# Transposing attention probabilities in fewer, larger groups

## The chip, the cores and the metric

The kernel runs on one core of one Trainium2 chip. The metric is the device time of one execution in microseconds (us). A core has five engines with a queue each: PE (TensorE, matmul and the loading of its weights, which the profile lists apart as PEld), ACT (ScalarE), DVE (VectorE), POOL (GpSimd) and SP (SyncE, which issues most of the DMA). The profile of one execution gives, for each instruction, its start, its duration and what it waited for.

## The reference

Two transformer blocks over 512 tokens and 1024 features, in float32. In order: a gated feed-forward layer; a mixer with two attentions side by side (a "forgetting" causal attention with 8 heads, and a "native sparse" one with 8 heads that adds a compressed, a selected and a windowed branch; at 512 tokens the selected and the windowed branch both come out as full causal attention); attention to 256 memory tokens with 4 heads of 256; a second feed-forward layer; sliding-window attention with sinks (16 heads, window 128); a pooling layer. Cut to what matters here, each attention is

```python
sc = jnp.einsum('bhqd,bkhd->bhqk', qi, k) + bias          # scores
p = masked_softmax(sc, mask)                               # rows are queries
o = jnp.einsum('bhqk,bkhd->bqhd', p.astype(v.dtype), v)    # products with the values
```

with a triangular mask in the mixer, none for the memory tokens, and a band of 128 in the window layer.

## The kernel before, in words

Activations lie feature-major, `[128 features, 512 tokens]`. Each large matmul is done three times to keep float32 accuracy: a number is split into a high part (ACT rounds it, L78) and a low part (DVE subtracts, L81), and `three` (L117 to L119) adds high*high, high*low and low*high. Weights come by DMA as `wr`, and are split into `wh` and `wl`; `wr`, `wh` and `wl` have three buffers each.

PSUM, where PE writes, has eight banks of `[128, 512]` in four pairs: `mm` (the large matmuls), `sc` (scores), `tr` (transposes, and a second bank for some matmuls) and `pv` (products with the values). Each name has two buffers: a third tile of that name waits until one of the two has been read for the last time.

An attention head is a `Unit` with three lists of steps: *scores*, *turns* and *products*. The probabilities come out of the softmax with queries on the partitions; for the product with the values they must have keys there. A *turn* transposes 128x128 blocks on PE into a `tr` bank, and ACT and DVE split that bank into `ph` and `pl`. A *product* multiplies `ph` and `pl` with the values.

- A causal unit (`causal_unit`, 24 of them: 8 in the forgetting attention, "fox", 16 in the native sparse one, "nsa") has four score steps, one for each block of 128 queries. Its four turns are one for each block j of 128 keys; only the blocks i >= j exist, so turn j has 4, 3, 2 or 1 transposes (L430) and its `ph` is 512, 384, 256 or 128 wide. Its four products (L442, L443) have two matmuls each.
- A memory unit (`mem_unit`, 4 of them) has two score steps and two turns of four transposes (L1015); all its product matmuls stand in its second product.
- A window unit (`swa_unit`, 16 of them) has two score steps, two turns of four and three transposes (L1193), and two products of eight and eight matmuls (L1209).

`run` sets the order on PE, by slots. One slot is: some steps of other work ("backlog": the matmuls of projections and gates that come later), one score step, at most one turn that has come due, some more backlog, at most one product that has come due. A unit's turns come due `lag` (2) slots after its last score, minus one, plus the unit's own `later`; a product comes due `hold` slots after its turn (1 in fox and in the memory layer, 2 in nsa and in the window layer). The backlog that is left is spread evenly over the slots that are left; `tail` says how many slots are counted on after the last score (6 in fox and nsa). `run` ends when no turn and no product is left. Work that is in the backlog then stays there, and goes out in the next `run` that has the same backlog; fox and nsa share one (`log` in `mixer`).

PE executes in exactly the order that is written. The order on ACT, DVE and POOL is made by a scheduler from the dependencies.

Other turns of the same kind in nsa: a unit for the compressed branch (`nsa_units`: L851 transposes its scores into a `tr` bank, which DVE reads at L853).

## Time and profile before

| | |
|---|---|
| median of 3 runs | 1718.14 us (1717.2 to 1718.44) |
| the profiled execution | 1718.07 us |
| its span, first to last instruction | 1716.3 us |
| outside the span | 1.8 us |
| granted TensorE clock, mean | 0.998 |
| busy: PE, PEld, DVE, ACT, POOL | 98%, 81%, 57%, 44%, 14% |
| fox run / nsa run / window run | about 438 to 548 / 573 to 745 / 1405 to 1512 us |
| the end of the memory run | 932 us |

A matmul's duration in the profile is the time from its start to the (modelled) end of its last write; consecutive matmuls overlap. What a matmul costs is therefore the distance from its start to the start of the next one: 0.23 us for a 512-wide matmul in a steady stream that has a duration of 0.40. A figure in square brackets behind a row is the idle time of the engine just before that instruction, and the instruction that ended it.

### The profile page before, as it was taken

The numbers are of one execution on the slowest core, as the hardware profiler recorded it, in microseconds if no ns is written. First come the engines' busy times: TensorE is split into PE (matmuls) and PEld (weight loads), VectorE is DVE, ScalarE is ACT, GpSimd is POOL, SyncE is SP. The second block draws the span as 40 slices with busy tenths as digits, with TensorE's granted clock in tenths as the row PEclk, the third lists the DMA queues.
The fourth block names the chain that finished last, engine by engine and source line by source line (L and its number), as shares of the span: only waits on it lengthen the run. The fifth ranks groups of instructions, "written<-read, shape, count | busy, mean of one in ns | idle before, by whom it ended". The sixth has DMA issues, their size and how long they took to land.

```text
span 1716.3 us, 22080 instructions
## 1 busy us (share of the span) xinstructions
PE 1683.8 (98%) x8300; PEld 1390.8 (81%) x8300; DVE 976.4 (57%) x1726; ACT 753.8 (44%) x1352; POOL 246.2 (14%) x323
## 2 busy tenths in 40 slices
PE   8999999999999999999999999999999999999997
PEld 5888878888787888887988888888888888878887
DVE  6343433336786677776655443433333698876674
ACT  6222222225675566645534432222223477744342
POOL 2000000003322232203001200000011044420001
PEclk9999999999999999999999999999999999999999
DMA  5222244433343122135521522222344311143232
GB/s 196 96 89 98 91 139 121 128 115 96 109 138 113 56 74 80 32 123 198 189 93 61 183 87 99 88 97 97 91 128 126 126 62 62 62 142 120 92 117 77
DMA packets 66256, 184.19 MB, mean 107 GB/s; under 512 B 7980, under 2 KB 13884, under 8 KB 66149
## 3 DMA queue, kind: packets, MB, share of 16 engines
q1 hardware_dynamic: 59300, 171.25, 30.9%
q10 hardware_dynamic: 6848, 11.54, 1.8%
q8 instruction: 65, 1.06, 0.2%
q14 instruction: 43, 0.34, 0.1%
HBM read 170.14 MB, written 15.24 MB: 108 GB/s over the span
## 4 chain that ended last, share of the span: by engine, by line
PE 88%; DVE 6%; ACT 2%; POOL 1%; issue 1%; DMA 0%; SPq 0%; DVEq 0%; ACTq 0%; POOLq 0%
PE mm L117 20%; PE mm L118 20%; PE mm L119 20%; PE tr L119 6%; PE tr L118 6%; PE tr L117 6%; PE tr L430 1%; PE pv L321 1%; DVE wl L81 1%; PE pv L322 1%; PE pv L323 1%; PE pv L443 1%; PE sc L403 1%; DVE pl L81 1%; PE pv L442 1%
## 5 line engine op out<-in xcount | busy, mean ns | idle before, releaser
L78 ACT ACTIVATE wh<-wr 128x1024 fp32r<-128x1024 f32 (+2 forms) x292 | 294.5, 1009 | 665.7 <-PE mm L118 351.4
L81 DVE TENSOR_TENSOR wl<-wr,wh 128x1024 fp32r<-128x1024 f32 (+2 forms) x291 | 342.5, 1178 | 172.9 <-ACT wh L78 168.7
L117 PE MATMUL mm<-xh,wh 128*128 128x512 f32 x872 | 358.3, 411 | 6.9 <-ACT wh L78 6.0
L118 PE MATMUL mm<-xl,wh 128*128 128x512 f32 x872 | 347.4, 398 | 0.9 <-DVE xl L89 0.7
L119 PE MATMUL mm<-xh,wl 128*128 128x512 f32 x872 | 346.3, 397 | 0.0
L223 POOL TENSOR_TENSOR acc<-acc,t 128x512 f32<-128x512 f32 (+1 forms) x55 | 75.3, 1376 | 958.8 <-ACT t L222 958.6
L117 PEld LDWEIGHTS mm<-xh,wh 128*128 128x128 f32 x872 | 166.0, 190 | 39.1 <-ACT wh L78 6.5
L119 PEld LDWEIGHTS mm<-xh,wl 128*128 128x128 f32 x872 | 164.8, 189 | 39.3 <-DVE wl L81 0.2
L118 PEld LDWEIGHTS mm<-xl,wh 128*128 128x128 f32 x872 | 165.5, 190 | 33.8 <-DVE xl L89 3.5
L119 PE MATMUL tr<-xh,wl 128*128 128x512 f32 x424 | 168.3, 397 | 0.5 <-DVE wl L81 0.5
L117 PE MATMUL tr<-xh,wh 128*128 128x512 f32 x424 | 168.2, 397 | 0.0
L118 PE MATMUL tr<-xl,wh 128*128 128x512 f32 x424 | 168.2, 397 | 0.0
L117 PE MATMUL mm<-hh,wh 128*128 128x512 f32 x352 | 139.0, 395 | 0.0
L119 PE MATMUL mm<-hh,wl 128*128 128x512 f32 x352 | 139.0, 395 | 0.0
L118 PE MATMUL mm<-hl,wh 128*128 128x512 f32 x352 | 139.0, 395 | 0.0
L356 DVE TENSOR_TENSOR t<-t,tr 128x512 f32<-128x512 f32 x44 | 30.2, 687 | 143.9 <-PE tr L119 142.5
L119 PEld LDWEIGHTS tr<-xh,wl 128*128 128x128 f32 x424 | 79.9, 189 | 20.3 <-DVE wl L81 0.9
L118 PEld LDWEIGHTS tr<-xl,wh 128*128 128x128 f32 x424 | 79.9, 189 | 19.4
L117 PEld LDWEIGHTS tr<-xh,wh 128*128 128x128 f32 x424 | 79.9, 188 | 19.3
L353 DVE TENSOR_TENSOR t<-mm,rstd 128x512 f32<-128x512 f32 x44 | 30.4, 691 | 112.4 <-PE mm L119 112.4
L81 DVE TENSOR_TENSOR pl<-tr,ph 128x512 fp32r<-128x512 f32 (+3 forms) x136 | 72.1, 530 | 24.0 <-ACT ph L78 23.1
L78 ACT ACTIVATE ph<-tr 128x512 fp32r<-128x512 f32 (+3 forms) x136 | 63.0, 466 | 50.8 <-PE tr L430 44.1
(346 smaller groups left out, 3000.8 us busy)
## 6 DMA issues: line engine op xcount, KB each, us to landing
wr<-in_f2gu_dram SPq DMA_DIRECT2D x44, 512.0 KB, 3.2
wr<-in_f1gu_dram SPq DMA_DIRECT2D x42, 512.0 KB, 3.3
wr<-in_mfm_dram SPq DMA_DIRECT2D x32, 512.0 KB, 3.2
xd<-xs ACTq DMA_DIRECT2D x40, 256.0 KB, 2.0
wr<-in_ain_dram SPq DMA_DIRECT2D x18, 512.0 KB, 3.2
wr<-in_f1d_dram SPq DMA_DIRECT2D x16, 512.0 KB, 3.7
xs<-xd SPq DMA_DIRECT2D x32, 256.0 KB, 3.3
wr<-in_f2d_dram SPq DMA_DIRECT2D x16, 512.0 KB, 3.6
```

Of the source, the lines that this page charges most:

```text
L78: nc.scalar.activation(o, i, AF.Copy, scale=scale)
L81: (eng or nc.vector).tensor_sub(o, i, h.bitcast(F32))
L117: nc.tensor.matmul(o, sh, mh, start=start, stop=False)
L118: nc.tensor.matmul(o, sh, ml, start=False, stop=False)
L119: nc.tensor.matmul(o, sl, mh, start=False, stop=stop)
L223: (nc.vector if last else nc.gpsimd).tensor_add(acc, acc, q[:, :n])
L321: mm(b, sh[k][:, tk], hi[:, c], start=first, stop=False, skip_group_check=True)
L322: mm(b, sh[k][:, tk], lo[:, c], start=False, stop=False, skip_group_check=True)
L323: mm(b, sl[k][:, tk], hi[:, c], start=False, stop=last, skip_group_check=True)
L353: nc.vector.tensor_mul(a, pg, r)
L356: nc.vector.tensor_mul(h, a, pu)
L403: nc.tensor.matmul(b[:, :n], q[:, c], kl[:, :n], start=False, stop=not diag)
```

## The change

In a causal unit the four turns become two. The first makes the transposes of j = 0 into one `tr` bank and those of j = 1 and j = 3 side by side into a second one (3 + 1 = 4 blocks), eight transposes in a row; then both banks are split. The second does j = 2 alone, two transposes. The products follow suit: one of six matmuls for j = 0, 1, 3 and one of two for j = 2. The split for j = 3 is gone as an instruction of its own: three pairs of ACT and DVE instructions instead of four.

In a memory unit and in a window unit the two turns become one, of eight and of seven transposes, in two banks; the two products become one. `later` is 1 there, so the one turn stands in the slot in which the second turn stood.

```diff
-        def turn(j):
+        def turn(group):
             def go():
                 pr = st["p"]
-                b = trb()
-                n = S - P * j
-                for i in range(j, NQ):
-                    nc.tensor.transpose(b[:, P * (i - j) : P * (i - j + 1)],
-                                        pr[:, OFF[i] + P * j : OFF[i] + P * (j + 1)], ident)
-                ph = pp.tile([P, S], F32R, tag="ph", bufs=3, name=nm("ph"))
-                pl = tp.tile([P, S], F32R, tag="xs", bufs=3, name=nm("pl"))
-                split(ph[:, :n], pl[:, :n], b[:, :n])
-                st[j] = ph[:, :n], pl[:, :n]
+                banks = []
+                for js in group:
+                    b = trb()
+                    at = 0
+                    for j in js:
+                        for i in range(j, NQ):
+                            nc.tensor.transpose(b[:, at : at + P],
+                                                pr[:, OFF[i] + P * j : OFF[i] + P * (j + 1)],
+                                                ident)
+                            at += P
+                    banks.append((js, b, at))
+                for js, b, n in banks:
+                    ph = pp.tile([P, S], F32R, tag="ph", bufs=3, name=nm("ph"))
+                    pl = tp.tile([P, S], F32R, tag="xs", bufs=3, name=nm("pl"))
+                    split(ph[:, :n], pl[:, :n], b[:, :n])
...
-        return Unit([score(i) for i in n4], [turn(j) for j in n4], [product(j) for j in n4], needs)
+        return Unit([score(i) for i in range(NQ)], [turn(((0,), (1, 3))), turn(((2,),))],
+                    [product((0, 1, 3)), product((2,))], needs)
...
-        return Unit([score(0), score(1)], [turn(0), turn(1)], [product(0), product(1)], needs)
+        return Unit([score(0), score(1)], [turn], [product], needs, 1)
```

(The last pair stands twice, for the memory unit and for the window unit.)

The change moves instructions on PE in three places that matter below. The names: `P` is the tile of a unit's probabilities, `tr`, `mm`, `sc`, `pv` are PSUM banks, `xh`, `xl` the activations, `vf` the values; the numbers tell tiles apart.

**The first causal unit of fox, PE.** Before:

```order
L430 MATMUL tr_3257<-ident,P_3118 128x128 x4
...
L430 MATMUL tr_3282<-ident,P_3118 128x128 x3
L117 MATMUL mm_3231<-xh_77,wh_3233 128x512
L118 MATMUL mm_3231<-xl_85,wh_3233 128x512
L119 MATMUL mm_3231<-xh_77,wl_3234 128x512
L442 MATMUL pv_3293<-ph_3262,vf 128x512
L443 MATMUL pv_3293<-pl_3263,vf 128x512
```

Now:

```order
L433 MATMUL tr_3257<-ident,P_3118 128x128 x4
L433 MATMUL tr_3262<-ident,P_3118 128x128 x4
...
L433 MATMUL tr_3291<-ident,P_3118 128x128 x2
L117 MATMUL mm_3231<-xh_77,wh_3233 128x512
L118 MATMUL mm_3231<-xl_85,wh_3233 128x512
L119 MATMUL mm_3231<-xh_77,wl_3234 128x512
L454 MATMUL pv_3301<-ph_3267,vf 128x512
L456 MATMUL pv_3301<-pl_3268,vf 128x512
L454 MATMUL pv_3301<-ph_3271,vf 128x384
L456 MATMUL pv_3301<-pl_3272,vf 128x384
L454 MATMUL pv_3301<-ph_3271,vf 128x128
L456 MATMUL pv_3301<-pl_3272,vf 128x128
```

The first product stands where it stood, and now reads two pairs of `ph` and `pl` instead of one.

**Between the fox run and the nsa run, PE.** Before, the backlog is empty at the end of the fox run (the last product of fox is the pair of L442 and L443):

```order
L117 MATMUL mm_4254<-xh_78,wh_4256 128x512
L118 MATMUL mm_4254<-xl_86,wh_4256 128x512
L119 MATMUL mm_4254<-xh_78,wl_4257 128x512
L565 MATMUL tr_4307<-hw_4056 64x64 x2
L442 MATMUL pv_4264<-ph_4290,vf 128x128
L443 MATMUL pv_4264<-pl_4291,vf 128x128
L117 MATMUL mm_4364<-xh_71,wh_4366 128x512
```

Now fox's `run` ends two slots earlier, when the last gate projection (`mm_4227`, weights `wh_4229`) has three of its eight steps behind it; its other five come in the first slots of the nsa run, behind three projections, each a bank of the name `mm`, and a projection of the values:

```order
L119 MATMUL mm_4227<-xh_73,wl_4230 128x512
L454 MATMUL pv_4237<-ph_4223,vf 128x256
L456 MATMUL pv_4237<-pl_4224,vf 128x256
L117 MATMUL mm_4298<-xh_71,wh_4300 128x512
...
L119 MATMUL mm_4298<-xh_78,wl_4301 128x512
L117 MATMUL mm_4335<-xh_71,wh_4337 128x512 [waits DVE_49]
...
L117 MATMUL mm_4376<-xh_71,wh_4378 128x512 [waits DVE_49,Activation_49]
...
L117 MATMUL mm_4227<-xh_74,wh_4229 128x512
```

The tile `mm_4227` stays open over all of that, and so does one of three buffers of `wh` and `wl`.

**The compressed unit of nsa behind a causal unit, PE** (second of four such units). Before:

```order
L851 MATMUL tr_5061<-ident,t_5040 128x64 x3
L430 MATMUL tr_5078<-ident,P_4934 128x128 [waits DVE_49,Pool_49]
L430 MATMUL tr_5078<-ident,P_4934 128x128 [waits Pool_49] x3
L117 MATMUL mm_5048<-ofh_2542,wh_5050 128x512
L118 MATMUL mm_5048<-ofl_2546,wh_5050 128x512
```

Now:

```order
L864 MATMUL tr_5000<-ident,t_4987 128x64 x3
L433 MATMUL tr_5017<-ident,P_4866 128x128 [waits PE_49,Pool_49]
L433 MATMUL tr_5017<-ident,P_4866 128x128 [waits Pool_49] x3
L433 MATMUL tr_5022<-ident,P_4866 128x128 [waits DVE_49]
L433 MATMUL tr_5022<-ident,P_4866 128x128 x3
L117 MATMUL mm_5035<-ofh_2541,wh_5037 128x512
```

The name `tr` has two banks. The compressed unit's transposes take one, the first four of the group the other, and the next four need the first one again.

## The prediction

> **What bounds the kernel now.** I read the page first (busy shares, the chain), then busy time in the four stages that the change touches, then the groups of instructions, and last PE's rows in order of time around the transposes.

> ```profile
> PE 1683.8 (98%) x8300; PEld 1390.8 (81%) x8300; DVE 976.4 (57%) x1726; ACT 753.8 (44%) x1352; POOL 246.2 (14%) x323
> PE 88%; DVE 6%; ACT 2%; POOL 1%; issue 1%; DMA 0%; SPq 0%; DVEq 0%; ACTq 0%; POOLq 0%
> ...
> 438.00:548.00 110.00, 105.90 (x588) 86.04 (x588) 88.21 (x186) 75.89 (x163) 29.25 (x41) 1.00 0.34 111
> 580.00:760.00 180.00, 179.12 (x944) 149.13 (x943) 129.10 (x360) 108.64 (x260) 42.28 (x84) 1.00 0.22 67
> 880.00:932.00 52.00, 51.18 (x276) 43.09 (x275) 28.87 (x45) 23.26 (x54) 7.06 (x14) 1.00 0.18 61
> 1405.00:1515.00 110.00, 105.78 (x603) 90.40 (x602) 94.99 (x261) 78.58 (x206) 47.19 (x63) 1.00 0.19 63
> ```

> The first two rows are busy time by engine and the chain's shares; the other four are stretches of time (fox, nsa, the end of the memory layer, the window layer) with PE's busy time first and the granted clock (1.00) third from the end. PE is the bound everywhere: it is idle for 4.1 + 0.9 + 0.8 + 4.2 = 10.0 us in these stages, out of 452. So the change can gain in two ways only: PE needs less time for its instructions, or it waits less. A freed ACT or DVE is worth nothing by itself; they are 55% to 86% busy here, so what matters of them is when, not how much.

> **The cost of a group of transposes.** The rows of PE around a group of four and a group of one; between them, the group's sum over the trace:

> ```profile
> 463.00 0.23 PE L405 MATMUL sc<-cmask_bf,ident_bf 128*128 128x128 bf16 x1
> 463.07 0.61 PE L430 MATMUL tr<-ident,P 128*128 128x128 f32 x4
> 463.43 0.48 PE L117 MATMUL mm<-xh,wh 128*128 128x512 f32 x1
> 463.75 0.40 PE L118 MATMUL mm<-xl,wh 128*128 128x512 f32 x1
> 463.98 0.39 PE L119 MATMUL mm<-xh,wl 128*128 128x512 f32 x1
> ...
> L430 PE MATMUL tr<-ident,P 128*128 128x128 f32 x240 | 44.0, 277 | 2.0 <-POOL P L420 1.5 <-DVE pl L81 0.5
> ...
> 474.00 0.28 PE L430 MATMUL tr<-ident,P 128*128 128x128 f32 x1
> 474.04 0.48 PE L117 MATMUL mm<-xh,wh 128*128 128x512 f32 x1
> 474.35 0.40 PE L118 MATMUL mm<-xl,wh 128*128 128x512 f32 x1
> ```

> A 512-wide matmul normally costs 0.23 (463.75 to 463.98). Right behind transposes it costs 0.32 (463.43 to 463.75) or 0.31 (474.04 to 474.35): about 0.09 more. That looks like a price for each change from transposes to matmuls, which larger groups would save. It is not, as the start of the group shows. Four transposes take 0.36 up to the next start, one takes 0.04. From the first transpose to the second start behind the group, less one normal matmul, four cost 463.75 - 463.07 - 0.23 = 0.45 and one costs 474.35 - 474.00 - 0.23 = 0.12. The difference is 0.33 for three, 0.11 each; so n transposes cost 0.11n + 0.01. What a group loses at its end, it has gained at its beginning, where its first weights are loaded under the long matmul before. Joining two groups saves 0.005 to 0.01, not 0.09. The change takes away 2 groups in each of 24 causal units and 1 in each of 20 others, 68 in all: **-0.3 to -0.7, I take -0.4**. The number of transposes and of product matmuls is the same (the group rows would show it), and the merged products are 512, 384 and 128 wide as before. The 24 splits of 128 columns that go away are ACT and DVE time, under PE.

> The distance of 0.11 is that of this trace. [...]

> **Waits that go away.** Three waits of PE before transposes:

> ```profile
> 519.30 0.23 PE L405 MATMUL sc<-cmask_bf,ident_bf 128*128 128x128 bf16 x1
> 520.01 0.33 PE L430 MATMUL tr<-ident,P 128*128 128x128 f32 x1 [0.48 <-DVE pl L81]
> ...
> 1416.32 0.28 PE L1158 MATMUL sc<-kt,q 128*128 128x256 f32 x1
> 1416.44 0.28 PE L1159 MATMUL sc<-kt,q 128*128 128x256 f32 x1
> 1417.43 0.99 PE L1193 MATMUL tr<-ident,pr 128*128 128x128 f32 x4 [0.72 <-DVE sm L1175]
> 1418.18 0.48 PE L117 MATMUL mm<-xh,wh 128*128 128x512 f32 x1
> ...
> 1436.27 0.28 PE L1159 MATMUL sc<-kt,q 128*128 128x256 f32 x1
> 1437.03 0.55 PE L1193 MATMUL tr<-ident,pr 128*128 128x128 f32 x3 [0.48 <-DVE pl L81]
> ```

> The first and the third wait for a `tr` bank that DVE has not read yet. With the new groups a bank has three slots (fox) or two full slots with no turn between (window) before it is needed again: gone, 0.71 - 0.07 = 0.64 (normal: 463.00 to 463.07) and 0.76 - 0.12 = 0.64 (normal: 1416.32 to 1416.44). The second is the window layer's first turn, for which the softmax is late: 0.99 - 0.12 = 0.87, and 0.75 - 0.36 = 0.39 inside the group. Its unit's turn now stands a slot later, where the second turn stood, and finds the softmax done. **-0.6 in fox, -1.9 in the window layer**; at worst the same waits come elsewhere (0).

> **Waits that are new.** (a) *The open bank at nsa's head.* `mm_4227` keeps one of two `mm` banks while three projections of 24 matmuls pass through the other. The second and the third must each wait until DVE has read the one before. How long that takes, from the last matmul's start:

> ```profile
> 543.32 0.40 PE L119 MATMUL mm<-xh,wl 128*128 128x512 f32 x1
> 543.75 0.69 DVE L613 TENSOR_TENSOR yf<-mm,rstd 128x512 f32<-128x512 f32 x1 [1.66 <-PE mm L119]
> L81 DVE TENSOR_TENSOR wl<-wr,wh 128x1024 fp32r<-128x1024 f32 (+2 forms) x291 | 342.5, 1178 | 172.9 <-ACT wh L78 168.7
> ```

> 0.43 + 0.69 = 1.12 instead of 0.23: 0.9 each, **+1.8**. The upper end is a weight split on DVE in front of each, 1.18 more: +4.2. On DVE's order only the second has a `wl` ahead of it, and that one can start when the first projection ends, 24 x 0.23 = 5.5 us earlier, so I stay at the lower end. The weights' third buffer is held as well; the other two turn over once in 5.5 us, enough for the ACT and DVE split.

> (b) *The bank behind the compressed unit.* In three places the second bank of the group of eight was just filled by the compressed unit's transposes (L851), and DVE must read it (L853) first:

> ```profile
> 653.32 0.69 DVE L619 SCALAR_TENSOR_TENSOR yf<-yf,mm 128x512 f32<-128x512 f32 x1 [0.78 <-PE mm L119]
> 653.60 0.66 PE L430 MATMUL tr<-ident,P 128*128 128x128 f32 x4
> 653.92 0.42 DVE L853 TENSOR_TENSOR pc<-tr,bc 128x256 f32<-128x256 f32 x1
> ```

> L853 ends at 654.34; the fifth transpose could start at 653.60 + 4 x 0.11 = 654.04. **+0.3 each, +0.9**; this is a case with another pass (L619) ahead on DVE. Bounds: 0, and 1.2 more each with a `wl` ahead (+4.5). Behind the waiting transposes stand backlog matmuls that need nothing from them; all of PE waits.

> (c) *The end of the memory layer*, where no backlog is left. Now and then:

> ```profile
> 923.35 0.60 PE L1015 MATMUL tr<-ident,pr 128*128 128x128 f32 x4
> 924.39 0.63 PE L1015 MATMUL tr<-ident,pr 128*128 128x128 f32 x4 [0.44 <-DVE pl L81]
> ...
> 927.16 0.60 ACT L78 ACTIVATE ph<-tr 128x512 fp32r<-128x512 f32 x1
> 927.79 0.69 DVE L81 TENSOR_TENSOR pl<-tr,ph 128x512 fp32r<-128x512 f32 x1
> ...
> 928.01 0.47 PE L117 MATMUL pv<-ph,vh 128*128 128x512 f32 x1
> 928.54 0.50 PE L118 MATMUL pv<-pl,vh 128*128 128x512 f32 x1
> ...
> 929.11 0.40 PE L117 MATMUL pv<-ph,vh 128*128 128x512 f32 x1
> 929.82 0.51 PE L118 MATMUL pv<-pl,vh 128*128 128x512 f32 x1 [0.32 <-DVE pl L81]
> ```

> Lost now: (1.04 - 0.36) + (0.53 - 0.32) + (0.71 - 0.23) = 1.4. With the change each of the last two heads goes eight transposes, then product, on PE. Counted from the first transpose: ACT and DVE first split the output of the product before (0.2 to 0.8 and 0.8 to 1.5), then `ph` 0.8 to 1.4, `pl` 1.5 to 2.2. PE is free at 0.9, waits for `ph` until 1.4 and, one matmul later (1.6), for `pl` until 2.2: 1.1 a head, 2.2 for two. **+0.8**; bounds 0 (the outputs split behind, not ahead) and +2.

> The merged product in fox needs two pairs of `ph` and `pl` at the time at which it needed one. From its first transpose to the merged product PE has 0.9 of transposes, 9 to 12 matmuls (2.1 to 2.8) and the next scores with two transposes (0.7): about 4. Two ACT copies and two DVE passes behind the bank's end at 0.6 (0.61 in the row at 463.07) end at 0.6 + 0.6 + 0.6 + 0.7 = 2.5, so 1.5 is left for what stands in front on ACT and DVE: **0** in the sum, and a rival.

> **The sum.** -0.4 - 0.6 - 1.9 + 1.8 + 0.9 + 0.8 = +0.6. Span 1716.3 + 0.6 = 1716.9; with the 1.8 outside it 1718.7 for an execution like the profiled one (1718.07), which is 0.07 below the median: **1718.8**. Less than 0.2% (3.4 us, about what a measurement of this kernel can tell from no change) either way is "the same".

> **Rivals.**

> 1. *Faster by relief.* ACT and DVE lose 24 splits and work in larger pieces with empty slots between; other waits of PE shorten too. For it: of the 10.0 us of idle PE only 2.5 (the 0.6 and the 1.9) are in my gains. Against it: most of the rest has other causes, such as `q` or the compression. If half of the idle time goes and the new waits are half of what I take: 1718.1 - 0.4 - 5.0 + 1.8 = **1714.5**.

> 2. *Slower by late products*, from the point at which ACT and DVE need over 4 us from the first transpose to the second `pl`. The place is fox, where a `hold` of 1 leaves one slot. For it:

> ```profile
> 470.71 0.44 PE L442 MATMUL pv<-ph,vf 128*128 128x384 f32 x1 [0.64 <-ACT ph L78]
> 472.08 0.45 PE L443 MATMUL pv<-pl,vf 128*128 128x384 f32 x1 [0.94 <-DVE pl L81]
> ```

> Here 1.6 went because the splits of a key projection stood ahead of one pair. If it happens in four of eight fox units to one more pair: 4 x 1.6 = 6.4, **1725**. Against it: the free 1.5 us above, and that it happened once in 32 products.

> 3. *Faster by spacing*: in a run of eight the loads of the weights run further ahead, and transposes start closer than in runs of four. The one row that has it is the single transpose with 0.04 to the next start. [...] Against it: the three steps inside a group of four are at the full 0.11.

> 4. *Slower at nsa's head*: both ends (a) and (b) at half of their upper bounds, +1.2 and +1.8 more: **1722**.

> That the change doesn't do what it says is excluded by PE's written order.

> **Chances.** No change 0.60 (forecast), rival 1 0.16, rival 3 0.03, rival 2 0.11, rival 4 0.10. Rivals 1 and 3 are faster, 2 and 4 slower: 0.19, 0.60, 0.21. The forecast's own bounds are 1714.7 to 1721.6; to leave no more than 2 in 10 out, the range takes in rivals 1 and 4: 1714 to 1723.

> **What would show it.** In the new trace: eight transposes followed by a 512-wide matmul of 0.32, 0.80 from the first start to that matmul (right: groups save nothing; wrong: under 0.7). No wait for DVE ahead of transposes in the window layer. Two waits of PE for DVE, about 0.9 each in start distance, some 5.5 us apart at nsa's head; three of about 0.3 behind L864. In the last two memory heads, waits for `ph` and `pl` of 1.1 together. I am wrong if fox's products wait for the second pair, or if PE's idle time in fox and in the window layer falls below 2 us each.

## The result: 1.2% slower, and the profile after

| | before | changed |
|---|---|---|
| median | 1717.67 us (4 runs, 1717.08 to 1718.44) | 1738.45 us (4 runs, 1735.46 to 1740.28) |
| ratio | | 1.0118, 95% interval 1.0106 to 1.0131 |
| span of the profiled execution | 1716.3 us | 1738.5 us |

The forecast was no change, 1714 to 1723. The time is 20.8 us above the kernel before. (One execution of a variant below, "later", ran slow, 1833.91 us at a clock of 0.85, and is left out of its median.) First the page of the changed kernel (span, busy time by engine, the chain's shares), then its PE in the same four stages as in the prediction (PE's busy time first, the granted clock third from the end):

```profile
span 1738.5 us, 22018 instructions
PE 1695.0 (97%) x8300; PEld 1398.2 (80%) x8300; DVE 972.1 (56%) x1702; ACT 749.0 (43%) x1328; POOL 244.3 (14%) x323
PE 85%; DVE 8%; ACT 3%; issue 1%; POOL 1%; DMA 1%; SPq 0%; DVEq 0%; ACTq 0%; POOLq 0%
...
438.00:548.00 110.00, 104.86 (x571) 85.78 (x570) 84.53 (x174) 72.09 (x149) 32.65 (x47) 0.98 0.35 117
580.00:760.00 180.00, 172.08 (x897) 141.79 (x896) 118.00 (x335) 102.37 (x240) 41.18 (x84) 0.99 0.18 56
900.00:957.00 57.00, 55.27 (x291) 46.05 (x290) 29.72 (x47) 23.53 (x54) 7.05 (x14) 1.00 0.17 56
1425.00:1535.00 110.00, 105.34 (x602) 90.77 (x601) 93.86 (x264) 78.89 (x207) 45.16 (x62) 0.98 0.17 58
```

PE's idle time is 43.5 (1738.5 - 1695.0) instead of 32.5, and most of the new idle time is in nsa: 7.9 of 180 instead of 0.9. But PE's busy time rose too, by 11.2, for the same 8300 matmuls. The last columns give one reason: the granted clock is no longer 1.00 in three of these stages. The other is in the waits themselves, whose beginning counts as busy because the matmul before is still on its way (an example follows). New waits and the clock need separate reading.

**New waits.** Three kinds, each with its rows. (1) The softmax is late for the group of eight. The last score of a unit and the group that needs it, in fox, before (first three rows) and changed (last four):

```profile
482.84 0.39 PE L402 MATMUL sc<-d,q 128*128 128x512 f32 x1
488.05 0.50 PE L430 MATMUL tr<-ident,P 128*128 128x128 f32 x3
489.18 0.33 PE L430 MATMUL tr<-ident,P 128*128 128x128 f32 x1 [0.63 <-POOL P L420]
```

```profile
484.27 0.39 PE L402 MATMUL sc<-d,q 128*128 128x512 f32 x1
488.74 0.39 PE L433 MATMUL tr<-ident,P 128*128 128x128 f32 x2
489.47 0.33 PE L433 MATMUL tr<-ident,P 128*128 128x128 f32 x1 [0.34 <-POOL P L420]
490.57 0.77 PE L433 MATMUL tr<-ident,P 128*128 128x128 f32 x5 [0.76 <-POOL P L420]
```

POOL's last rows of probabilities are there 6.3 behind the score both times (489.18 - 482.84, 490.57 - 484.27). What changed is when PE comes: after 5.2 before, after 4.5 now. The group stands as many slots behind the last score as ever, but in the slots between stood the transposes and products of the unit before, and most of those have moved to earlier slots. PE runs through the gap faster and waits at its end. Over the eight units of fox the mean distance from last score to first transpose fell from 5.8 to 5.1. The rows also show what a wait costs: from 489.47 to 490.57 PE has one transpose, which normally costs 0.11, so 0.99 is lost, of which 0.76 is idle; the rest counts as busy.

(2) The group of two comes one slot behind the group of eight, which has both `tr` banks. In nsa, PE and then DVE:

```profile
607.80 1.04 PE L433 MATMUL tr<-ident,P 128*128 128x128 f32 x8
611.30 0.44 PE L433 MATMUL tr<-ident,P 128*128 128x128 f32 x2 [1.41 <-DVE pl L81]
...
608.80 0.69 DVE L81 TENSOR_TENSOR q<-t,q 64x512 fp32r<-64x512 f32 x1
610.56 1.27 DVE L81 TENSOR_TENSOR pl<-tr,ph 128x512 fp32r<-128x512 f32 x2
```

DVE begins to read the banks only at 610.56, with a split of `q` and softmax steps ahead. (3) The three places that the prediction had named do wait: nsa's open bank, the bank behind the compressed unit, the memory units' end (rows below, with the prediction's points).

**Half clock.** Stretches of 3.41 us on the changed kernel, two pairs in a row (PE busy first, clock third from the end):

```profile
631.87:635.28 3.41, 1.35 (x8) 1.11 (x9) 1.64 (x7) 1.20 (x4) 2.08 (x4) 1.00 0.30 77
635.28:638.69 3.41, 3.41 (x11) 2.75 (x11) 2.49 (x5) 1.38 (x4) 0.00 (x0) 0.50 0.00 0
823.02:826.43 3.41, 0.64 (x3) 0.44 (x4) 3.06 (x6) 3.39 (x6) 1.81 (x2) 1.00 0.54 162
826.43:829.84 3.41, 3.41 (x10) 2.65 (x10) 2.38 (x4) 1.45 (x3) 0.83 (x1) 0.50 0.64 208
...
636.22 0.63 PE L118 MATMUL mm<-ofl,wh 128*128 128x512 f32 x1
636.64 0.63 PE L119 MATMUL mm<-ofh,wl 128*128 128x512 f32 x1
```

In the first stretch of each pair PE waited and had little to do, 1.35 and 0.64 of 3.41; the *next* 3.41 us then ran at a clock of 0.50, with matmuls of 512 columns 0.43 apart instead of 0.23 (last two rows). 3.41 us of that hold what takes 3.41 x 0.23 / 0.43 = 1.8 at full clock, so such a window, or half-clock window as it is called below, costs about 1.6 by this estimate (the expectations below take half of 3.41, 1.71, which is a little too much). The changed kernel has four inside its span (from 505.6, 635.3, 826.4 and 1475.0), the profile before none. By PE's start distances they cost 1.4 to 1.6 each: 6.1 of the 22.2 by which the span grew.

### The profile page after: what moved, and what is told of

Read it like the earlier page. It is cut to its first block, busy times and chain, and to the rows that moved or that the text cites. A ratio compares the mean times of both kernels' runs of the same rounds, so it can differ in the third digit from the quotient of the medians.

```text
span 1738.5 us, 22018 instructions
## 1 busy us (share of the span) xinstructions
PE 1695.0 (97%) x8300; PEld 1398.2 (80%) x8300; DVE 972.1 (56%) x1702; ACT 749.0 (43%) x1328; POOL 244.3 (14%) x323
## 4 chain that ended last, share of the span: by engine, by line
PE 85%; DVE 8%; ACT 3%; issue 1%; POOL 1%; DMA 1%; SPq 0%; DVEq 0%; ACTq 0%; POOLq 0%
PE mm L117 19%; PE mm L118 19%; PE mm L119 18%; PE tr L119 6%; PE tr L117 6%; PE tr L118 6%; DVE wl L81 2%; PE pv L321 1%; PE tr L433 1%; PE pv L322 1%; PE pv L323 1%; PE pv L456 1%; POOL P L420 1%; DVE pl L81 1%; PE pv L454 1%
## 5 line engine op out<-in xcount | busy, mean ns | idle before, releaser
L78 ACT ACTIVATE wh<-wr 128x1024 fp32r<-128x1024 f32 (+2 forms) x292 | 294.6, 1009 | 666.9 <-PE mm L118 348.5
L81 DVE TENSOR_TENSOR wl<-wr,wh 128x1024 fp32r<-128x1024 f32 (+2 forms) x291 | 343.2, 1180 | 175.0 <-ACT wh L78 170.4
L117 PE MATMUL mm<-xh,wh 128*128 128x512 f32 x872 | 356.6, 409 | 9.2 <-ACT wh L78 6.0
L118 PE MATMUL mm<-xl,wh 128*128 128x512 f32 x872 | 348.1, 399 | 0.2
L119 PE MATMUL mm<-xh,wl 128*128 128x512 f32 x872 | 347.4, 398 | 0.0
L117 PEld LDWEIGHTS mm<-xh,wh 128*128 128x128 f32 x872 | 166.0, 190 | 44.2 <-ACT wh L78 6.6
L119 PEld LDWEIGHTS mm<-xh,wl 128*128 128x128 f32 x872 | 165.4, 190 | 39.8 <-DVE wl L81 0.2
L118 PEld LDWEIGHTS mm<-xl,wh 128*128 128x128 f32 x872 | 166.0, 190 | 34.5 <-DVE xl L89 2.3
L119 PE MATMUL tr<-xh,wl 128*128 128x512 f32 x424 | 168.2, 397 | 0.3 <-DVE wl L81 0.3
L117 PE MATMUL tr<-xh,wh 128*128 128x512 f32 x424 | 168.1, 396 | 0.0
L118 PE MATMUL tr<-xl,wh 128*128 128x512 f32 x424 | 168.1, 396 | 0.0
L117 PE MATMUL mm<-hh,wh 128*128 128x512 f32 x352 | 138.9, 395 | 0.0
L118 PE MATMUL mm<-hl,wh 128*128 128x512 f32 x352 | 138.9, 395 | 0.0
L119 PE MATMUL mm<-hh,wl 128*128 128x512 f32 x352 | 138.9, 395 | 0.0
L119 PEld LDWEIGHTS tr<-xh,wl 128*128 128x128 f32 x424 | 79.9, 188 | 20.2 <-DVE wl L81 0.8
L118 PEld LDWEIGHTS tr<-xl,wh 128*128 128x128 f32 x424 | 79.9, 188 | 19.5
L117 PEld LDWEIGHTS tr<-xh,wh 128*128 128x128 f32 x424 | 79.9, 188 | 19.3
L118 PEld LDWEIGHTS mm<-hl,wh 128*128 128x128 f32 x352 | 66.3, 188 | 15.5
L119 PEld LDWEIGHTS mm<-hh,wl 128*128 128x128 f32 x352 | 66.3, 188 | 15.5
```

The lines of the kernel that those rows point to most:

```text
L78: nc.scalar.activation(o, i, AF.Copy, scale=scale)
L81: (eng or nc.vector).tensor_sub(o, i, h.bitcast(F32))
L117: nc.tensor.matmul(o, sh, mh, start=start, stop=False)
L118: nc.tensor.matmul(o, sh, ml, start=False, stop=False)
L119: nc.tensor.matmul(o, sl, mh, start=False, stop=stop)
```

## The experiments

For each stage the table below gives the time that PE *lost* in it: the sum, over the stage's matmuls, of the distance to the next start less the usual distance for a matmul of that shape (its median in the kernel before: 0.23 for 512 columns, 0.12 for 256, 0.11 for a transpose of 128x128). This counts each wait whole, and it does not depend on which matmuls stand in the stage. The length of a stage does: the open backlog moves 15 matmuls (3.5 us) from fox into nsa in the full change and with fox alone, and 6 with "later" and with "gap"; and where nsa's own run ends early, it hands 3 or 6 on to the next stage. "Half clock" is what was lost in half-clock windows, counted apart (their number in brackets, without those at the very end). All this is of the profiled execution. "Time" is the difference of medians from the kernel before on the same chip. Fox and nsa's head reach from fox's first score to nsa's first causal score, nsa to its last product, memory from its first score to the first matmul behind its last product, the window layer from its first score (1379.8 in the kernel before) to its last product.

| kernel | fox and nsa's head | nsa | nsa to memory | memory | window | half clock | time, us |
|---|---|---|---|---|---|---|---|
| before | 7.4 | 2.3 | 2.7 | 1.7 | 6.4 | 0 | 0 |
| full change | 11.3 | 12.8 | 4.2 | 3.2 | 6.2 | 6.1 (4) | +20.8 |
| fox alone | 11.4 | 4.8 | 2.9 | 1.6 | 6.1 | 1.4 (1) | +7.2 |
| nsa alone | 7.4 | 8.4 | 2.7 | 1.6 | 6.1 | 0 | +4.8 |
| memory alone | 7.4 | 2.3 | 2.7 | 3.2 | 6.5 | 0 | +0.8 |
| window alone | 7.4 | 2.3 | 2.8 | 1.7 | 6.4 | 1.4 (1) | -0.3 |
| full, tail 4 | 15.8 | 8.4 | 2.8 | 3.2 | 6.4 | 7.9 (5) | +24.2 |
| full, later | 11.2 | 5.6 | 2.7 | 3.1 | 6.5 | 3.1 (2) | +10.6 |
| full, gap | 9.7 | 5.3 | 4.2 | 3.1 | 6.5 | 6.0 (4) | +11.3 |
| full, later and gap | 10.0 | 0.5 | 2.8 | 3.2 | 6.5 | 4.3 (3) | +3.5 |
| fox and nsa, later and gap, hold 2 | 9.8 | 0.5 | 2.7 | 1.6 | 6.4 | 1.6 (1) | +2.5 |
| before, tail 5 | 12.7 | 2.3 | 2.7 | 1.6 | 6.6 | 2.8 (2) | +7.0 |
| full, tail 4, split on POOL | 14.4 | 8.5 | 2.6 | 3.2 | 6.2 | 6.1 (4) | +20.7 |
| nsa alone, later and gap | 7.6 | 0.5 | 2.7 | 1.6 | 6.1 | 2.9 (2) | -0.7 |

### One part of the change at a time

Each takes one of the four parts from the changed kernel and the other three from the kernel before (for fox and nsa, `causal_unit` gets its groups as an argument).

> Only the eight causal units of fox are regrouped; nsa, memory and window units are as before. Theory A (lost slack and half-clock windows, formed from the changed kernel's trace: the group of eight starts as many slots behind the last score as before, but the slots between hold less work now, so the softmax is late; and where a 3.41 us window holds too little matmul work, the next one runs at half clock and costs 1.71): fox's waits go from 5.1 to between 5.8 and 7.5, and nsa's head gets two waits of about 1.0 for the open bank; 2.5 to 6 us slower than before. Theory B (the sum of the prediction): -0.6 in fox, -0.15 for groups, +1.8 at nsa's head; about 1 us slower.

> Only the sixteen causal units of nsa are regrouped; fox, memory and window units are as before. Theory A (lost slack, bank too early for the group of two, half-clock windows): waits for POOL ahead of the group of eight and for DVE ahead of the group of two, 2.0 now, 8 to 10 then, and one or two half-clock windows of 1.71; 6 to 12 us slower. Theory B (the prediction): +0.9 behind the compressed unit, -0.15 for groups; within 1 us of before.

> Only the four memory units are merged; all else is as before. Theory A and B agree on the place (the last two heads, products directly behind the transposes): A +1.4 by the changed kernel's trace, B +0.8 by the prediction's working; 0.5 to 1.5 us slower. Over 2 us would speak for a cause that neither has.

> Only the sixteen window units are merged; all else is as before. Theory A: the waits for q at three places and the one late softmax stay, they only move; 5.8 before, 5.5 to 6.0 now, plus one half-clock window (1.71) where a wait of about 2 falls into one 3.41 us window; 0 to 2.5 us slower. Theory B (the prediction): -1.9 because the late softmax and the bank wait go; about 2 us faster.

Measured, as ratios to the kernel before: fox 1.0041 (1.0028 to 1.0053), nsa 1.0026 (1.0016 to 1.0037), memory 1.0006 (0.9997 to 1.0015), window 1.0000 (0.9992 to 1.0009). Theory B is out for fox, for nsa and for the window layer. Theory A set fox too low and nsa too high. Fox alone costs more than its own waits: of the 4.0 more in the first column 2.0 are the two waits at nsa's head, and with fox alone the *unchanged* units of nsa lose 2.5 more too, by waits for POOL, since the moved matmuls shift nsa's backlog. The memory units lose 1.5 in their stage, but as a time their 0.8 can't be told from no change. And the parts do not add up: 7.2 + 4.8 + 0.8 - 0.3 = 12.5 of 20.8. In nsa the two causes, 2.5 with fox alone and 6.1 with nsa alone, make 10.5 together, and the full change has four half-clock windows where the parts have two. The window layer's waits only moved: the first softmax wait and the bank wait went (the prediction's 1.9), and a later unit's softmax and `q` are later instead; the changed kernel has them too:

```profile
1457.12 0.98 PE L1201 MATMUL tr<-ident,pr 128*128 128x128 f32 x7 [1.29 <-DVE sm L1184]
1473.99 0.33 PE L1167 MATMUL sc<-kt,q 128*128 128x128 f32 x1 [2.05 <-DVE q L81]
```

### Giving back the slots

All four are the full change with one edit. Tail 4 edits the call of `run` in fox:

```diff
-                    run(units, log, hold=1)
+                    run(units, log, tail=4, hold=1)
```

The others edit the last lines of `causal_unit` (the scores are unchanged; shown here written in place, in the runs the groups and the 1 come in as an argument). Later:

```diff
-                    [product((0, 1, 3)), product((2,))], needs)
+                    [product((0, 1, 3)), product((2,))], needs, 1)
```

Gap, a turn and a product that do nothing between the two; later and gap has the 1 at its end as well:

```diff
-                    [turn(((0,), (1, 3))), turn(((2,),))],
-                    [product((0, 1, 3)), product((2,))], needs)
+                    [turn(((0,), (1, 3))), lambda: None, turn(((2,),))],
+                    [product((0, 1, 3)), None, product((2,))], needs)
```

> The full change, with one number more: the fox run counts on 4 slots after its last score instead of 6, which is how many it now has, so its backlog is empty at its end and no bank stays open at nsa's head. Theory A (lost slack, bank too early, half-clock windows): the two waits of 0.95 at nsa's head go, and what the 15 moved matmuls brought into nsa goes with them (nsa's waits from 12.7 towards the 6.9 of the run with nsa alone); of the 20.8 of the full change 13 to 18 are left. Rival (the open bank is only worth its two waits): 18.5 to 19.5 are left.

> The full change, with both turns of every causal unit one slot later (later = 1). Theory A: the group of eight starts a slot of about 3 us later behind the last score, so its waits for POOL (2.4 in fox, about 6 in nsa in the changed kernel's trace) go, and with them a half-clock window or two; the waits of the group of two for DVE (about 4 in nsa) stay; of the 20.8 of the full change 8 to 13 are left. Rival (POOL and DVE are late because they have more to do at once, not because the group comes early): the same waits stand a slot later, 17 or more are left.

> The full change, with an empty slot between the group of eight and the group of two of every causal unit. Theory A: DVE has two slots instead of one to read the two banks, so the waits for DVE ahead of the group of two (0.35 in fox, about 4 in nsa) go; the waits for POOL ahead of the group of eight stay, a little smaller, because work moves back between them; of the 20.8 of the full change 13 to 17 are left. Rival (DVE is simply busy at that time): the waits move to the products, 19 or more are left.

> The full change, with both turns of every causal unit one slot later and an empty slot between the group of eight and the group of two. The group of two then stands in the slot in which the last turn stood before, and the fox run ends as before with an empty backlog. Theory A: all three causes are gone, what is left is the memory units' 0.8 and a half-clock window now and then: -1 to +4 against the kernel before. Rival (a run of eight transposes, two banks and two pairs to split at once is itself what delays ACT and DVE): +8 or more.

Later 1.0063 (1.0049 to 1.0078), gap 1.0068 (1.0055 to 1.0081), both 1.0024 (1.0014 to 1.0033): the rivals are out, though the gap gave more than expected. With the slot later, no wait for POOL ahead of a group of eight is left in fox or nsa; with the empty slot, none of the group of two for DVE. With both, nsa loses less than before, 0.5 against 2.3, and PE is idle for 0.2 of the 180 that hold it:

```profile
438.00:548.00 110.00, 104.28 (x571) 84.89 (x569) 83.77 (x173) 71.44 (x148) 29.42 (x41) 0.98 0.32 108
580.00:760.00 180.00, 179.82 (x954) 151.90 (x953) 129.69 (x357) 106.24 (x247) 41.51 (x85) 1.00 0.21 66
```

Each of the two edits also gives fox one of its two lost slots back, so a part of their gain in nsa can be due to the fewer moved matmuls. The table's last row leaves that out: with fox as before, nsa alone loses 8.4 in nsa, and 0.5 with the later slot and the empty one. So in nsa the lost slots are the cause, shown by taking them away and by giving them back. Fox, in the first row above, is not cured: 5.7 idle of 110.

Tail 4 went against every theory: 1.0147 (1.0130 to 1.0163), more than the full change. Half of the expectation held: nsa's head has its two waits no more, and nsa's loss fell to 8.4, what it is with nsa alone. But in fox the loss grew to 15.8. Its longest wait, on PE, and DVE at that time:

```profile
470.91 0.44 PE L433 MATMUL tr<-ident,P 128*128 128x128 f32 x2 [3.19 <-DVE pl L81]
...
465.88 1.23 DVE L81 TENSOR_TENSOR wl<-wr,wh 128x1024 fp32r<-128x1024 f32 x1
467.02 3.05 DVE L81 TENSOR_TENSOR kl<-t,d 64x512 fp32r<-64x512 f32 x3
470.10 0.17 DVE L415 RECIPROCAL sm<-sm 128x2 f32<-128x2 f32 x1
470.18 1.27 DVE L81 TENSOR_TENSOR pl<-tr,ph 128x512 fp32r<-128x512 f32 x2
```

A weight split and three splits of the key projection, 4.2 in a row, stand ahead of `pl`. That raised a new question: is it the regrouping that fox can't bear, or does fox's time hang on where these bursts fall?

### Fox: the regrouping, or the place of the bursts

The first of these three has fox and nsa regrouped, with the later slot and the empty one, and gives fox's products one slot more (memory and window units as before). The second regroups nothing: the kernel before with `tail=5` in fox's `run`. The third is tail 4 with one of the three key splits moved from DVE to POOL.

```diff
-            low(lo[e][other, :], t[rows, :], pair[e][rows, :], nc.gpsimd if e else None)
+            low(lo[e][other, :], t[rows, :], pair[e][rows, :], nc.gpsimd)
```

> Both fox and nsa regrouped, a slot later and with the empty slot; fox's products in addition one slot later (a hold of 2 instead of 1); memory and window units as before. Theory A (fox's products wait because a burst of key splits on DVE stands ahead of pl, and one slot more covers it): fox's waits fall from 8.7 in the run with both later to about 5.6, the value of the kernel before; 1.5 faster to 1 slower than before. Rival (the same burst then holds up the transposes or the scores instead): 2 to 5 slower.

> The kernel before, nothing regrouped; the fox run counts on 5 slots after its last score instead of 6, so its backlog is a little denser per slot and empty a slot earlier. Theory of placement (fox's waits hang on where DVE's bursts fall against the slots, and the kernel before is well placed): fox's waits, 5.6 before, change by 2 or more; 2 to 8 slower. Rival (only the regrouping makes fox wait): 5 to 6.5 of waits, within 1 of the kernel before.

> The full change with the fox run counting on 4 slots, and one of the three DVE splits of each key projection (about 1.0 each) moved to POOL. Theory of the burst: the wait of the group of two for pl at 31 us into fox falls from 3.35 to about 2.3, and fox's waits from 17.2 by 1.5 to 5; 20 to 23 above the kernel before, instead of 24. Rival (POOL then is the one that is late, with the softmax's last step): waits for POOL ahead of the group of eight grow by as much; 24 or more.

Hold 2: 1.0013 (1.0004 to 1.0021); fox and head lose 9.8, about as without it (10.0). The waits of the products are gone, and others stand in their place; the rival holds. The longest:

```profile
502.89 0.39 PE L544 MATMUL mm<-wh,st 128*128 128x256 f32 x1 [3.02 <-DVE u L551]
```

Tail 5 without any regrouping: 1.0039 (1.0027 to 1.0052), 7.0 slower; fox and head lose 12.7 instead of 7.4, and there are two half-clock windows. One number in the backlog's density, and the kernel before loses as much as regrouping fox costs, though not in the same places: with fox alone 2.0 of the 4.0 in this column stand at nsa's head, and nsa loses 2.5. The three longest waits of tail 5, all at products; of the first there was 0.94 in the kernel before, of the others none:

```profile
472.87 0.45 PE L456 MATMUL pv<-pl,vf 128*128 128x384 f32 x1 [1.70 <-DVE pl L81]
...
489.08 0.38 PE L454 MATMUL pv<-ph,vf 128*128 128x256 f32 x1 [1.97 <-ACT ph L78]
491.21 0.39 PE L456 MATMUL pv<-pl,vf 128*128 128x256 f32 x1 [1.74 <-DVE pl L81]
```

So fox's waits hang on where the slots put its work, and the loss in it changes by 5.3 without any regrouping; that is shown. With every edit of fox's slots tried here PE lost more in fox than in the kernel before, which suggests that its placement happens to be a good one. It is not shown that any other edit would lose, nor what larger groups would cost in fox at an equally good placement.

The split on POOL: 1.0117 (1.0103 to 1.0130), 20.7 above before instead of 24.2, within the range expected. But the named wait grew, from 3.35 to 4.18 (in start distance), where 2.3 was expected. DVE and POOL, tail 4 (the second row is the last of the three splits of the first) and, in the next block, with the split moved:

```profile
467.02 3.05 DVE L81 TENSOR_TENSOR kl<-t,d 64x512 fp32r<-64x512 f32 x3
468.43 1.64 DVE L81 TENSOR_TENSOR kl<-t,d 64x512 fp32r<-64x512 f32 x1
467.80 1.72 POOL L81 TENSOR_TENSOR kl<-t,d 64x512 fp32r<-64x512 f32 x1 [3.41 <-ACT d L78]
```

```profile
466.90 3.44 DVE L81 TENSOR_TENSOR kl<-t,d 64x512 fp32r<-64x512 f32 x2
466.32 3.47 POOL L81 TENSOR_TENSOR kl<-t,d 64x512 fp32r<-64x512 f32 x2 [2.69 <-ACT d L78]
```

Two splits took DVE longer than three did, 3.44 against 3.05. In tail 4 the first two took 0.68 each, and only the third, which began at 468.43 with POOL's one under way since 467.80, took 1.64; with the split moved POOL has two of its own at that time, and DVE's two take 3.44 together. The burst did not get shorter, so that wait could not. Fox loses 1.4 less all the same, and has one half-clock window fewer (1.8); where the 1.4 comes from was not settled.

### The half clock, and a faster kernel

The clock was tested where PE waits for the norm of the memory tokens. 12 matmuls into an unread bank ahead of its first matmul, and 8 ahead of its second, fill the waits (shortened; for this norm alone):

```diff
         b = scb()
+        d = pvb()
+        for z in range(12):
+            nc.tensor.matmul(d[:, :n], ones_r, busy, start=True, stop=True)
         nc.tensor.matmul(b[:, :n], ones_r, ah, start=True, stop=False)
+        for z in range(8):
+            nc.tensor.matmul(d[:, :n], ones_r, busy, start=True, stop=True)
         nc.tensor.matmul(b[:, :n], ones_r, al, start=False, stop=True)
```

This went into the full change, into the kernel before, and into the kernel before with nsa alone regrouped, later and with the gap (that one also without it, and with `look=2` instead of 1 in the window layer's `run`).

> The full change, with 12 and 8 matmuls of 256 columns into a bank that nobody reads, ahead of the two matmuls of the memory tokens' norm (L253, L254), where PE waits 2.5 and 1.4 in the changed kernel's trace and 1.4 and 1.2 in the kernel before. Theory of windows (a 3.41 us window with less than about 1.4 to 1.8 of matmul work makes the next one run at half clock): this place never shows half clock again, and costs no time of its own, since the added matmuls (1.4 and 0.9) run inside the waits; 0 to 1.7 less than the full change, 19 to 20.8 above the kernel before. Rival (the clock falls for a reason other than the idle of that place, such as the load of the whole core): half clock still follows this wait, and the time is that of the full change or up to 2 more.

> The kernel before with the 12 and 8 added matmuls at the memory tokens' norm alone. Theory of windows: the half clock behind this wait goes from those executions that had it, 0.3 to 1.2 less than the kernel before, and the regrouping in nsa has the rest of the 1.9 that it and the added matmuls gained together. Rival: all of the 1.9 is here and regrouping gains nothing; 1.7 to 2.2 less.

> The kernel before, with the regrouping in nsa alone, a slot later and with an empty slot between the group of eight and the group of two; fox, memory and window units are as before. Theory A: nsa's waits fall from 2.0 to 0.4, as in the last run, and 32 groups fewer save 0.2; 1.5 to 2 us faster than before. Rival (the later products push something behind nsa): no faster, 0 to +2.

> The run with nsa alone, a slot later and with the empty slot, and the same 12 and 8 added matmuls at the memory tokens' norm. Theory of windows: no half clock behind this norm in any execution; 0.3 to 1.7 less than without the added matmuls, since only a part of the executions has the half clock there. Rival (other reasons for the clock): 0, or up to 2 more, for the matmuls added.

> Nsa regrouped with the slot later and the empty slot, the added matmuls at the memory tokens' norm, and in the window layer each q projection asked for one slot earlier (look 2 instead of 1); window units not regrouped. If the window layer's waits for q (0.84 + 1.41 + 0.65 + 1.15 in the run without it) are the projection's lateness alone, they go: 3 to 4 less than without it, 1711.5 to 1713. Rival (DVE is the one that is late, whatever the order on PE): the waits stay, 1715 to 1717.

The full change with the added matmuls: 1.0102 (1.0086 to 1.0117), 16.4 above before. That is 4.4 less, more than the one half-clock window (about 1.6) that the place can give. Its profiled execution has no half clock at all before the end, and that includes three places that were not touched. One of them, the wait for POOL in nsa, with the two windows in which it falls:

```profile
631.01 0.33 PE L440 MATMUL tr<-ident,P 128*128 128x128 f32 x1 [2.19 <-POOL P L427]
...
626.60:630.01 3.41, 2.22 (x13) 1.72 (x11) 3.35 (x9) 2.23 (x6) 0.00 (x0) 1.00 0.00 0
630.01:633.43 3.42, 2.08 (x11) 1.69 (x12) 1.62 (x7) 1.69 (x4) 2.07 (x4) 1.00 0.31 77
```

The same wait is 2.21 in the full change, in a stretch with 1.35 of PE work, and has a half-clock window behind it; here it lies across two stretches, with 2.22 and 2.08 of PE work, and the clock stays at 1.00. That this is the reason is the author's reading of these rows. The mean clocks of the other executions agree, but for one of the three: the executions of the full change had 0.994, 0.994, 0.995 and 0.996, at 1740.3, 1739.3, 1737.6 and 1735.5; of this one 0.998, 0.995, 0.997 and 0.997. One window takes 0.001 off the mean clock (half of 3.41, of 1738). So the clock agrees with the theory of windows; the size of the gain, from four executions each, is partly a matter of where the half clock fell in each.

The others: the kernel before with added matmuls 0.9996 (0.9987 to 1.0005); nsa alone with later and gap 0.9999 (0.9990 to 1.0008); that with added matmuls 0.9989 (0.9980 to 0.9998). The two singles can't be told from no change, so they decide nothing between theory and rival; the pair is 0.1% faster than before. In the traces nsa loses 1.8 less (0.5 against 2.3), but half-clock windows that come and go hide as much: two in the profile without the added matmuls, none in the one with them.

With `look=2`: 1711.15 us, ratio 0.9954 (0.9940 to 0.9968). This beats both kernels. The window layer loses 2.8 instead of 6.4; one of four waits for `q` is left (0.86), and two waits for POOL (0.5 and 1.7 in start distance) have come:

```profile
1430.97 0.33 PE L1216 MATMUL tr<-ident,pr 128*128 128x128 f32 x1 [0.36 <-POOL pr L1202]
1492.97 0.33 PE L1216 MATMUL tr<-ident,pr 128*128 128x128 f32 x1 [1.51 <-POOL pr L1202]
```

Of its 7.1 us the greater part has nothing to do with the change studied here.

## Why the prediction was wrong

The terms of the sum against the time that PE lost in the profiled execution, changed less before:

| place | term | measured |
|---|---|---|
| fewer groups | -0.4 | in their stages |
| fox | -0.6 | +1.9 |
| nsa's head, (a) | +1.8 | +2.0 |
| behind the compressed unit, (b) | +0.9 | +1.1 |
| the rest of nsa | 0 | +9.4 |
| nsa to memory | 0 | +1.4 |
| end of the memory layer, (c) | +0.8 | +1.5 |
| window layer | -1.9 | -0.3 |
| half clock | 0 | +6.1 |
| all other stages | 0 | -0.9 |
| sum | +0.6 | +22.2 |

So (a), (b), (c) and the window layer came out within their bounds, fox did not, and most of the loss is where the sum had nothing: in the rest of nsa and in the clock. The 1.4 between nsa and memory is a longer wait at the memory tokens' norm (L253, L254), and why it is longer was not looked into.

**Right, and by its own terms.** The cost of a group: eight transposes take 0.80 to the next start and that matmul 0.31, as expected; rival 3 (closer spacing) is out, since the seven steps inside this group are 0.11 each:

```profile
451.69 1.04 PE L433 MATMUL tr<-ident,P 128*128 128x128 f32 x8
452.49 0.47 PE L117 MATMUL mm<-xh,wh 128*128 128x512 f32 x1
452.80 0.40 PE L118 MATMUL mm<-xl,wh 128*128 128x512 f32 x1
```

Term (a), the open bank, +1.8: 0.94 and 1.04 at nsa's head, 6.8 apart. Term (b), the compressed unit's bank, +0.9: 0.41, 0.41 and 0.27 in three places, 1.1 (one of them is the start distance of 1.21 instead of 0.80 here):

```profile
550.42 0.50 PE L117 MATMUL mm<-xh,wh 128*128 128x512 f32 x1 [0.78 <-DVE t L620]
557.18 0.47 PE L117 MATMUL mm<-xh,wh 128*128 128x512 f32 x1 [0.88 <-DVE t L618]
...
664.49 1.45 PE L433 MATMUL tr<-ident,P 128*128 128x128 f32 x8
665.70 0.47 PE L117 MATMUL mm<-ofh,wh 128*128 128x512 f32 x1
```

Term (c), the end of the memory layer, +0.8: its waits are 2.7 instead of 1.4, and the stage loses 1.5 more; each of the last two heads waits as worked out (0.54 for `ph`, 0.51 to 0.52 for `pl`), and a third wait for `pl` of 0.62 ahead of them was not in the sum.

**Where it failed.** Four places.

1. "With the new groups a bank has three slots (fox)". The transposes and the splits were counted, the slots were not: the group of two needs a bank *one* slot behind the group of eight. The sum has no term for it. In nsa it is a wait of 0.5 to 1.6 at four places of the full change, 4.0 together. The run with the empty slot showed it.

2. Of the causal units the sentence was that the first product "stands where it stood". So it does, by slots. The prediction took a slot as a length of time; but a slot is as long as what stands in it, and the change emptied the slots between the last score and the group. The sum put this at nothing; in nsa the waits for POOL ahead of transposes grew from 1.6 to 5.8. No rival had a late softmax in fox or nsa, though the row of 0.63 behind POOL at 489.18 in the kernel before, one of the 10.0 of idle time left as having "other causes", showed that there was no slack. The run a slot later showed it.

3. "-1.9 in the window layer". "At worst the same waits come elsewhere (0)" is, but for 0.3, what happened.

4. The clock was read as 1.00 everywhere, and no term priced what a wait can do to the matmuls behind it. At four places of the changed kernel 3.41 us at a clock of 0.50 came behind such waits and cost 1.4 to 1.6 each. This was 6.1 in the profiled execution, over a quarter of the loss.

Term (a) had a second half that was missed: the moved matmuls cost nsa 2.5 even with its old groups. Rival 2 (fox's merged products wait for the second pair) did not come: one product of fox waits, for 1.2, and it is the last one of its unit, not a merged one. What makes fox wait is that its bursts on DVE fall differently after a shift of the slots, as tail 5 showed without a regrouping. These mechanisms push one way, and the sum had been made of single waits at known places; the bounds were bounds of those places only.

Three readings ahead of the result were off, without weight in the sum: ACT is busy for 23.26 of 52 at the end of the memory layer, which is 45% and not 55% or more; the window layer begins at 1379.8, so the stretch from 1405 leaves out its first 25 us; and each product of a window unit has four matmuls, not eight.

## What to carry to other kernels

In an order made of slots, a change that moves work between slots changes the slots' lengths. Before counting what an edit saves, list for every producer how long after its input the consumer comes, in time and not in slots, and see what fills that time after the edit. A schedule on which PE is 98% busy has little spare time to move a wait to: expect a reordering to lose at first, and look for the compensating edit (here one slot later and one empty slot) before judging the idea. And price PE's waits beyond their own length: in the changed kernel four places with waits that left PE 0.64 to 1.36 of work in 3.41 us had half clock behind them, 1.4 to 1.6 more each.

## What was not expected of the hardware

**DVE and POOL at once.** In tail 4, three subtractions of 64x512 took DVE 3.05 with one such on POOL, from 467.80 to 469.52: the first two 0.68 each, the third, from 468.43, 1.64. With two on POOL at that time, which took 3.47, two took DVE 3.44, 1.72 each on the mean. So the move of a split from DVE to POOL made DVE's burst 0.4 longer here, where both were busy at the same time; why a subtraction takes longer then was not shown.
